# Products of the weights-stationary jobs sent in four runs of one width per block, and a lock for holders of several 512-column slots

## The chip, the cores and the metric

The kernel runs on one core of a Trainium2 chip. The metric is the time of one execution in device microseconds (us); less is better. The comparison is with the kernel before, whose median over three runs is 1254.39 us. Two engines matter most here: TensorE (PE in the profile), which multiplies, with its weight loads shown as PEld; and VectorE (DVE), which does the additions, differences and sums between the products. ScalarE (ACT) copies, rounds and applies functions; SyncE (SP) starts the transfers of the weights.

## The reference

Two layers of a decoder trunk over 256 positions and 1024 channels, in float32. Each layer is a mixer and a feed-forward part:

```python
u = rmsnorm(h) @ w_in                       # q, k, v, g, z, xbc, dt and two gates
yr = retention(rotary(q), rotary(k), v)      # 4 heads, chunks of 128
o_ret = (silu(g) * yr * rsqrt(mean(yr**2))) @ ret_out
xs, bm, cm = split(silu(causal_dwconv(xbc)))
ys = ssd_scan(xs * dt, dt * a, bm, cm)       # 4 groups of 8 heads, chunks of 128
o_ssd = (norm(ys + d_skip * xs, silu(z))) @ ssd_out
h = h + (sigmoid(gr) * o_ret + sigmoid(gs) * o_ssd) @ w_o
h = h + (silu(f @ w_gate) * (f @ w_up)) @ w_down     # f = rmsnorm(h)
```

and a last rmsnorm. Nearly all of the arithmetic is in the products with weights, some 260 MB of which are read once.

## The kernel before

**Products.** Every float32 operand of a large product is split into a high part (`wh` of a weight piece, `xh` of an activation) and the rest (`wl`, `xl`), and three products stand for one: high by high, high by low, low by high. In most jobs the activations are the stationary operand and TensorE streams 512 columns of weights three times (`mm3`, L541 to L543).

**The weights-stationary jobs** (`fm_job`, L971) turn this round. They make the projections that are needed with channels on the partitions: bc, q, k and xs in the mixer, and part of gate and up in the feed-forward. The stationary operand is 128x128 of weights, and what is streamed is the activation `xT`, whose tile keeps high and low halves side by side (256 + 256 columns). So one product of 512 columns with `wh` gives high by high and high by low at once (L989, or L992 for the last), and one of 256 columns with `wl` gives low by high (L990), added into the first 256 columns of the same PSUM bank. A job has two blocks (`b`) of 128 output channels; a block is eight k-steps, each a 512 and a 256, in turn. Its weights come in two pieces (k 0 to 3 and k 4 to 7), each of which must have been split by ScalarE (`wh`, L504) and VectorE (`wl`, L525). A layer has 30 such jobs (4 bc, 4 q, 4 k, 8 xs, 10 in the feed-forward), so the program has 60 jobs and 120 blocks.

**What sets the order.** While the program is built, a planner (`Flow`, L72) plays all engines on a clock of its own. Work is written as streams, which ask for operations with a cost and a priority, for events and for slots (`Sem`). Whenever an engine is free, its ready operation of lowest priority number is emitted (`run`, L157). Each engine's order is thereby fixed at build time; on the chip every engine runs its own list, and waits for the others by semaphores. A k-step of `fm_job` is one operation of the planner (L995), and transposes, scores or the products of another stream can be put between two of them.

**512-column slots.** `sxS` (L262) has four buffers of 128x512. Several kinds of work take more than one at a time. `seven_sums` (L673) makes the sums of operand quarters that a seven-product scheme needs; where it has no ready copies (its `plain` is None), it fills all four (`plain<-Y` in the profile) and makes from them four sums (`plain<-plain`), each split in two. `ssd_chunk` (L1683) of the state-space scan takes two, `xdt` and `tail`, for each of the two chunks of a group; the first chunk's `xdt` is kept until the second has used it. Single slots go to the convolution (L1614), the retention scores (L1460) and `copied` (L905).

Of the kernel before, what the change touches and what calls it, by code (L numbers as in the profile page):

```python
# [18 lines left out]
SEQ = 256  # L19
# [173 lines left out]
def trunk_kernel(  # L193
# [35 lines left out]
    def tt(n, pr, out, in0, in1, op):  # L229
        return dve(n, pr, lambda: nc.vector.tensor_tensor(out=out, in0=in0, in1=in1, op=op))  # L230
# [14 lines left out]
    def pe(cost, pr, fn):  # L245
        return Op("pe", cost, fn, pr)
# [5 lines left out]
    def pooled(pool_, shape, dt, tag, bufs):  # L252
        sem = Sem(bufs)
        return sem, lambda name=tag: pool_.tile(list(shape), dt, tag=tag, name=name, bufs=bufs)
# [5 lines left out]
    ccS, new_cc = pooled(tp, (P, D), F32, "cc", 2)  # L260
    silS, new_sil = pooled(tp, (P, 512), F32, "sil", 3)
    sxS, new_sx = pooled(tp, (P, 512), F32, "sx", 4)  # L262
    segS, new_seg = pooled(tp, (P, HPG, P), F32, "seg", 2)
    wbS, new_wb = pooled(tp, (P, D), F32, "wb", 1)
    decS, new_dec = pooled(tp, (P, D), F32, "dec", 2)
# [407 lines left out]
    def seven_sums(ops, op, parts, tag, pr, plain=None):  # L673

        p, r = parts
        for q, n, t in (("11", p, 0), ("21", r, 0), ("t4", r, 1)):
            yield op.ready[n][t]
            fl.set(ops[q], tuple(a[:, :, t * P : (t + 1) * P] for a in op.at(n)[:2]))
        x = {}
        for n in range(2):  # L680
            for t in range(NT):
                yield (plain[n][t] if plain else op.ready[parts[n]][t])
        for n in range(2):
            for t in range(NT):
                if plain:
                    x[n, t] = yield plain[n][t]
                else:
                    xh, xl = (a[:, :, t * P : (t + 1) * P] for a in op.at(parts[n])[:2])
                    yield sxS
                    x[n, t] = new_sx("plain")  # L690
                    v = x[n, t].rearrange("p (j t) -> p j t", j=4)
                    yield tt(512, pr, v, xh.bitcast(F32), xl.bitcast(F32), ALU.add)
        x11, x12, x21, x22 = x[0, 0], x[1, 0], x[0, 1], x[1, 1]
        pair = None
        for i, (q, out, a, b, op_) in enumerate((
                ("t1", x22, x21, x22, ALU.subtract), ("t2", x22, x22, x11, ALU.subtract),
                ("22", x12, x12, x22, ALU.add), ("t3", x21, x11, x21, ALU.subtract))):
            yield tt(512, pr, out, a, b, op_)
            if i % 2 == 0:
                yield bigS[tag]  # L700
                yield bigS[tag]
                pair = new_big(tag, F32R), new_big(tag, F32R)
            sh, sl = (p[:, :, (i % 2) * P : (i % 2 + 1) * P] for p in pair)
            v = out.rearrange("p (j t) -> p j t", j=4)
            yield act(512, pr, sh, v, AF.Copy)
            yield tt(512, pr, sl, v, sh.bitcast(F32), ALU.subtract)
            fl.set(ops[q], (sh, sl))
        for _ in range(4):
            fl.release(sxS)
# [261 lines left out]
    def fm_job(xT, post):  # L971

        j, pe_pr = take()
        evs = jobs[j]
        second = Event()
        for b in range(2):
            fsl = slice(b * P, (b + 1) * P)
            yield accS
            ps = None
            for k in range(8):  # L980
                for t in range(NT):
                    yield xT.ready[k // 4][t]
                wh, wl = yield evs[k // 4]

                def emit():
                    a = new_acc() if ps is None else ps
                    xh, _, x = xT.at(k // 4)
                    if k < 7:
                        nc.tensor.matmul(a, lhsT=wh[:, k % 4, fsl], rhs=x[:, k % 4, :, :], start=k == 0, stop=False)  # L989
                    nc.tensor.matmul(a[:, :SEQ], lhsT=wl[:, k % 4, fsl], rhs=xh[:, k % 4, :], start=False, stop=False)  # L990
                    if k == 7:
                        nc.tensor.matmul(a, lhsT=wh[:, k % 4, fsl], rhs=x[:, k % 4, :, :], start=False, stop=True)  # L992
                    return a

                ps = yield pe(mm_cost(512) + mm_cost(256) + 5, pe_pr + 0.5, emit)  # L995
                if b == 1 and k % 4 == 3:
                    fl.release(hlS)
            if b == 0:
                fl.spawn(post(ps, second, j))
            else:  # L1000
                fl.set(second, ps)
# [260 lines left out]
    def layer(l, mix, nxt, opening=None):  # L1262
# [420 lines left out]
        def ssd_chunk(g, t, lp, pr, dtt, acs, dec, dr, prm, cb, xs, x0_ev):  # L1683
# [18 lines left out]
            yield Op("act", HPG * (0.833 * P + 185), differences, lp)  # L1702
            yield act(1024, lp, sg, sg, AF.Exp, scale=-1.0)
            yield tt(1024, lp, sg, sg, cb[:, 2 * t, :].unsqueeze(1).broadcast_to([P, HPG, P]), ALU.mult)
            yield sxS
            xdt = new_sx("xdt")
            yield tt(512, lp, h3(xdt), h3(xs[:, t, :]), hb(dtt, t * NH, g), ALU.mult)
            yield sxS
            tail = new_sx("tail")
            dsb = prm[:, 2, g * HPG : (g + 1) * HPG].unsqueeze(2).broadcast_to([P, HPG, HD])  # L1710
            yield tt(512, lp, h3(tail), h3(xs[:, t, :]), dsb, ALU.mult)
# [562 lines left out]
```

## Time and profile before

| | us |
|---|---|
| median of three runs | 1254.39 (1253.65 to 1254.71) |
| the profiled execution | 1252.77 |
| its span, first to last instruction | 1251.0 |
| TensorE busy | 1241.2 (99%) |
| VectorE busy | 1109.2 (89%) |
| ScalarE busy | 883.5 (71%) |

The profile is of one execution. A matmul's record lasts from its start to its modelled end, and the next starts before that, so mean durations overlap; what a matmul costs in a stream is the distance from its start to the next start. In a timeline the columns are start, duration (both us), engine, line, operation and operands. In groups they are the count, the busy time in us, the mean duration in ns, and the idle time before with what ended it. Lines (L...) are those of the kernel before.

### The profile page before, as it was taken

The page shows a single profiled execution, that of the slowest core. Times are in us where ns is not written, and L with a number is a line of the kernel's source. Part 1 is how long each engine was busy: PE and PEld are TensorE (multiplying, and loading weights), DVE is VectorE, ACT ScalarE, POOL GpSimd, SP SyncE. Part 2 cuts the span into 40 slices and gives each one's busy share as a digit, 9 for nine tenths or more (in the row PEclk, how much of TensorE's full clock was granted, in tenths as well). Part 3 has the DMA queues.
Part 4 walks back from the last instruction along what each step waited for, and adds up shares of the span by engine and source line. Part 5 has one row for each costly group of instructions (what it writes and reads, how often), then busy time and mean ns, then how long its engine had stood idle before and what let it go on. Part 6 is the DMA issues. An engine that isn't in the chain of part 4 may idle for free.

```text
span 1251.0 us, 17642 instructions
## 1 busy us (share of the span) xinstructions
PE 1241.2 (99%) x6301; PEld 1052.5 (84%) x6301; DVE 1109.2 (89%) x1520; ACT 883.5 (71%) x1307; POOL 71.1 (6%) x92
## 2 busy tenths in 40 slices
PE   9999999999999999999999999999999999999997
PEld 8889888888888888888888898888888888888886
DVE  6998989789999979999788888888899998889996
ACT  6866876977776666776586676878877674776753
POOL 0000000001012001001000000000010110010000
PEclk9999999999999999999999999999999999999999
DMA  8758555466768658877776574555576786678872
GB/s 300 246 141 284 184 181 173 153 199 187 252 239 224 230 178 230 295 217 218 250 255 225 123 259 163 189 170 163 210 187 234 243 234 213 217 212 254 292 201 88
DMA packets 76343, 266.27 MB, mean 213 GB/s; under 512 B 8768, under 2 KB 9280, under 8 KB 76256
## 3 DMA queue, kind: packets, MB, share of 16 engines
q1 hardware_dynamic: 68416, 237.39, 55.1%
q0 software_dynamic: 7552, 27.38, 11.7%
q8 instruction: 49, 0.80, 0.3%
q10 hardware_dynamic: 288, 0.39, 0.1%
q14 instruction: 38, 0.31, 0.1%
HBM read 262.96 MB, written 2.16 MB: 212 GB/s over the span
## 4 chain that ended last, share of the span: by engine, by line
PE 88%; ACT 4%; issue 3%; DMA 3%; DVE 2%; POOL 0%; SPq 0%; POOLq 0%; ACTq 0%; DVEq 0%
PE acc L541 19%; PE acc L543 19%; PE acc L542 18%; PE acc L989 14%; PE acc L990 8%; PE tr L638 2%; PE yps L1731 2%; PE acc L992 2%; ACT wh L504 2%; DMA raw<-in_w_fm_dram 1%; DMA raw<-in_w_tm_dram 1%; DVE wl L525 1%; ACT seg L1699 1%; PE acc L1453 1%; PE tr L1624 1%
## 5 line engine op out<-in xcount | busy, mean ns | idle before, releaser
L504 ACT ACTIVATE wh<-raw 128x1024 fp32r<-128x1024 f32 (+2 forms) x388 | 397.0, 1035 | 148.6 <-PE acc L543 33.2
L525 DVE TENSOR_TENSOR wl<-raw,wh 128x1024 fp32r<-128x1024 f32 (+2 forms) x388 | 457.9, 1193 | 48.2 <-ACT wh L504 46.3
L989 PE MATMUL acc<-xT,wh 128*128 128x512 f32 x840 | 304.1, 400 | 0.0
L990 PE MATMUL acc<-xT,wl 128*128 128x256 f32 x960 | 251.6, 281 | 0.0
L541 PE MATMUL acc<-wh,xT 128*128 128x512 f32 (+1 forms) x568 | 220.5, 388 | 0.0
L543 PE MATMUL acc<-wh,xT 128*128 128x512 f32 (+1 forms) x568 | 216.1, 381 | 0.0
L542 PE MATMUL acc<-wl,xT 128*128 128x512 f32 (+1 forms) x568 | 216.1, 380 | 0.0
L990 PEld LDWEIGHTS acc<-xT,wl 128*128 128x128 f32 x960 | 181.2, 189 | 10.1
L989 PEld LDWEIGHTS acc<-xT,wh 128*128 128x128 f32 x840 | 158.0, 188 | 32.1
L542 PEld LDWEIGHTS acc<-wl,xT 128*128 128x128 f32 x568 | 106.8, 188 | 20.5 <-issue 1.2
L541 PEld LDWEIGHTS acc<-wh,xT 128*128 128x128 f32 x568 | 106.8, 188 | 19.8 <-issue 1.6
L543 PEld LDWEIGHTS acc<-wh,xT 128*128 128x128 f32 x568 | 106.6, 188 | 19.4
L504 ACT ACTIVATE wh<-raws 128x1024 fp32r<-128x1024 f32 x80 | 83.6, 1057 | 32.3 <-DVE raws L230 11.3
L525 DVE TENSOR_TENSOR wl<-raws,wh 128x1024 fp32r<-128x1024 f32 x80 | 96.2, 1219 | 8.6 <-ACT wh L504 8.4
L541 PE MATMUL acc<-wh,A 128*128 128x512 f32 x224 | 89.8, 401 | 0.3
L543 PE MATMUL acc<-wh,A 128*128 128x512 f32 x224 | 87.4, 390 | 0.0
L542 PE MATMUL acc<-wl,A 128*128 128x512 f32 x224 | 87.3, 390 | 0.0
L233 DVE SCALAR_TENSOR_TENSOR cc<-cc,cv 128x255 f32<-128x255 f32 (+1 forms) x144 | 67.0, 476 | 3.0 <-ACT cc L223 2.1
L541 PE MATMUL acc<-wh,C 128*128 128x512 f32 (+2 forms) x155 | 59.7, 385 | 0.0
L542 PE MATMUL acc<-wl,C 128*128 128x512 f32 (+2 forms) x155 | 58.9, 380 | 0.4 <-DVE wl L525 0.4
L543 PE MATMUL acc<-wh,C 128*128 128x512 f32 (+2 forms) x155 | 58.8, 379 | 0.0
L223 ACT ACT_TABLE_LOAD x41 | 52.6, 1283 | 6.0 <-DVE cc L233 5.3
(197 smaller groups left out, 2008.1 us busy)
## 6 DMA issues: line engine op xcount, KB each, us to landing
raw<-in_w_tm_dram SPq DMA_DIRECT2D x104, 512.0 KB, 4.2
raw<-in_w_fm_dram SPq DMA_DIRECT2D x80, 512.0 KB, 4.1
raw<-in_w_gf_dram SPq DMA_DIRECT2D x40, 512.0 KB, 4.6
raw<-in_w_gate_up_dram SPq DMA_DIRECT2D x32, 512.0 KB, 5.9
raw<-in_w_down_dram SPq DMA_DIRECT2D x28, 512.0 KB, 4.6
raw<-in_w_gr_dram SPq DMA_DIRECT2D x24, 352.0 KB, 3.4
seg<-acs SPq DMA_DIRECT2D x16, 512.0 KB, 4.8
raw<-in_ret_out_dram SPq DMA_DIRECT2D x16, 512.0 KB, 4.3
```

The costliest lines, as they stand in the source:

```text
L223: return Op("act", cost, lambda: nc.scalar.activation(out=out, in_=in_, func=func, **kw), pr, TABLES.get(func))
L233: return Op("dve", 1.04 * n + 130, lambda: nc.vector.scalar_tensor_tensor(out=out, in0=in0, scalar=scalar, in1=in1, op0=op0, op1=op1), pr)
L504: nc.scalar.activation(out=wh[:, :m], in_=raw[:, :m], func=AF.Copy)
L525: nc.vector.tensor_tensor(out=wl[:, :m], in0=raw[:, :m], in1=wh[:, :m].bitcast(F32), op=ALU.subtract)
L541: nc.tensor.matmul(ps, lhsT=lh, rhs=rh, start=first, stop=False, **kw)
L542: nc.tensor.matmul(ps, lhsT=lh, rhs=rl, start=False, stop=False, **kw)
L543: nc.tensor.matmul(ps, lhsT=ll, rhs=rh, start=False, stop=last, **kw)
L638: nc.tensor.transpose(out=ps[:, j * P : (j + 1) * P], in_=src[:, j * P : (j + 1) * P], identity=ident)
L989: nc.tensor.matmul(a, lhsT=wh[:, k % 4, fsl], rhs=x[:, k % 4, :, :], start=k == 0, stop=False)
L990: nc.tensor.matmul(a[:, :SEQ], lhsT=wl[:, k % 4, fsl], rhs=xh[:, k % 4, :], start=False, stop=False)
L992: nc.tensor.matmul(a, lhsT=wh[:, k % 4, fsl], rhs=x[:, k % 4, :, :], start=False, stop=True)
L1731: nc.tensor.matmul(ps[:, i * HD : (i + 1) * HD], lhsT=sg[:, i, :], rhs=xdt[:, i * HD : (i + 1) * HD], start=True, stop=True)
```

## The change

Three things change in the code.

- In `fm_job` a block's products are sent in four runs: the four 512s of the first piece, its four 256s, the four 256s of the second piece, and its four 512s. Each run is given to the planner as two operations of two products each, and the planner's cost for them has 5 ns added for a pair of 512s and none for a pair of 256s (it was 5 ns for each 512 with its 256). A weight piece is given back at the same place as before, after its eighth product in the second block.
- A lock `sxG` with one holder. `seven_sums` takes it, where it has no ready copies, before its four slots, and gives it back when it has filled all four.
- `ssd_chunk` takes the same lock in a group's first chunk ahead of `xdt`, and it is given back in the second chunk when that has its second slot.

Nothing is added to or taken from the arithmetic: the numbers of products, additions and transfers are the same.

```diff
     sxS, new_sx = pooled(tp, (P, 512), F32, "sx", 4)
+    sxG = Sem(1)
...
             for t in range(NT):
                 yield (plain[n][t] if plain else op.ready[parts[n]][t])
+        if not plain:
+            yield sxG
...
                     yield tt(512, pr, v, xh.bitcast(F32), xl.bitcast(F32), ALU.add)
+        if not plain:
+            fl.release(sxG)
...
             yield accS
-            ps = None
-            for k in range(8):
+            box = []
+            for half, wide in ((0, True), (0, False), (1, False), (1, True)):
                 for t in range(NT):
-                    yield xT.ready[k // 4][t]
-                wh, wl = yield evs[k // 4]
-
-                def emit():
-                    a = new_acc() if ps is None else ps
-                    xh, _, x = xT.at(k // 4)
-                    if k < 7:
-                        nc.tensor.matmul(a, lhsT=wh[:, k % 4, fsl], rhs=x[:, k % 4, :, :], start=k == 0, stop=False)
-                    nc.tensor.matmul(a[:, :SEQ], lhsT=wl[:, k % 4, fsl], rhs=xh[:, k % 4, :], start=False, stop=False)
-                    if k == 7:
-                        nc.tensor.matmul(a, lhsT=wh[:, k % 4, fsl], rhs=x[:, k % 4, :, :], start=False, stop=True)
-                    return a
-
-                ps = yield pe(mm_cost(512) + mm_cost(256) + 5, pe_pr + 0.5, emit)
-                if b == 1 and k % 4 == 3:
+                    yield xT.ready[half][t]
+                wh, wl = yield evs[half]
+
+                def emit(k0):
+                    if not box:
+                        box.append(new_acc())
+                    xh, _, x = xT.at(half)
+                    for k in (k0, k0 + 1):
+                        if wide:
+                            nc.tensor.matmul(box[0], lhsT=wh[:, k, fsl], rhs=x[:, k, :, :],
+                                             start=(half, k) == (0, 0), stop=(half, k) == (1, 3))
+                        else:
+                            nc.tensor.matmul(box[0][:, :SEQ], lhsT=wl[:, k, fsl], rhs=xh[:, k, :], start=False, stop=False)
+
+                for k0 in (0, 2):
+                    yield pe(2 * mm_cost(512 if wide else SEQ) + (5 if wide else 0), pe_pr + 0.5, lambda: emit(k0))
+                if b == 1 and (half, wide) in ((0, False), (1, True)):
                     fl.release(hlS)
...
             yield act(1024, lp, sg, sg, AF.Exp, scale=-1.0)
+            if t == 0:
+                yield sxG
             yield sxS
             xdt = new_sx("xdt")
...
             yield sxS
+            if t == 1:
+                fl.release(sxG)
             tail = new_sx("tail")
```

How the change moves instructions is seen in the order in which each engine's list is emitted. Operands in it are named as in the profile, and a number after a name tells buffers apart. In the changed kernel's list L996 and L999 are the 512s and the 256s of `fm_job`, and L526 is the split that was L525.

TensorE, the first block of the first bc job, before: `wh_418` and `wl_459` are the first piece's high and low part, `wh_446` and `wl_470` the second's.

```order
L989 MATMUL acc_502<-xT_317,wh_418 128x512
L990 MATMUL acc_502<-xT_317,wl_459 128x256
L989 MATMUL acc_502<-xT_342,wh_446 128x512
L990 MATMUL acc_502<-xT_342,wl_470 128x256
L990 MATMUL acc_502<-xT_342,wl_470 128x256 x2
L992 MATMUL acc_502<-xT_342,wh_446 128x512
```

Of the rows that repeat one stands here; in the list the first two come four times and the next two three times. The same block and the next one in the changed kernel:

```order
L996 MATMUL acc_502<-xT_317,wh_418 128x512 x4
L999 MATMUL acc_502<-xT_317,wl_459 128x256 x4
L999 MATMUL acc_502<-xT_342,wl_470 128x256 x4
L996 MATMUL acc_502<-xT_342,wh_446 128x512 x4
L996 MATMUL acc_537<-xT_317,wh_418 128x512 x4
L999 MATMUL acc_537<-xT_317,wl_459 128x256 x4
L999 MATMUL acc_537<-xT_342,wl_470 128x256 x4
L996 MATMUL acc_537<-xT_342,wh_446 128x512 x4
```

The width changes fourteen times inside a block before, and twice in the changed kernel; from one block to the next 512 follows 512 in both.

VectorE in layer 0, where the retention's sums begin and the second chunk of a state-space group ends, before: `plain<-Y` fills a slot for `seven_sums`, `xdt<-ips`, `tail<-tail` and `C<-yps` belong to the chunk, `wl<-raw` splits a weight piece, `sil<-A` and `A<-tr` make the retention's output.

```order
L230 TENSOR_TENSOR xdt<-ips,sr 128x512
L230 TENSOR_TENSOR tail<-tail,xdt 128x512
L233 SCALAR_TENSOR_TENSOR sil<-A,rr_2068,sil 128x512
L230 TENSOR_TENSOR plain<-Y 128x512
L233 SCALAR_TENSOR_TENSOR sil<-A,rr_2068,sil 128x512
L525 TENSOR_TENSOR wl<-raw,wh 128x1024
L230 TENSOR_TENSOR C<-yps,tail 128x512
L230 TENSOR_TENSOR plain<-Y 128x512
L230 TENSOR_TENSOR A<-tr,A 128x4x128
L230 TENSOR_TENSOR plain<-Y 128x512 x2
```

The same place in the changed kernel, from the same first row on:

```order
L230 TENSOR_TENSOR xdt<-ips,sr 128x512
L230 TENSOR_TENSOR tail<-tail,xdt 128x512
L230 TENSOR_TENSOR Y<-tr,Y 128x4x128
L233 SCALAR_TENSOR_TENSOR cc<-cc,cv 128x255
L230 TENSOR_TENSOR plain<-Y 128x512
L233 SCALAR_TENSOR_TENSOR cc<-cc,cv 128x254
L526 TENSOR_TENSOR wl<-raw,wh 128x1024
L233 SCALAR_TENSOR_TENSOR cc<-cc,cv 128x253
L526 TENSOR_TENSOR wl<-raw,wh 128x1024
L230 TENSOR_TENSOR cc<-acc,cc 128x256
L230 TENSOR_TENSOR C<-yps,tail 128x512
L230 TENSOR_TENSOR plain<-Y 128x512
```

The chunk's product sum `C<-yps` is still behind the first slot that `seven_sums` fills, with more convolution rows and one more weight split between; the four fills are drawn out over more of VectorE's list.

More of the change, by code (lines that the diff above doesn't have):

```diff
@@ L978, in fm_job @@
             yield accS
-            ps = None
-            for k in range(8):
+            box = []
+            for half, wide in ((0, True), (0, False), (1, False), (1, True)):
                 for t in range(NT):
-                    yield xT.ready[k // 4][t]
-                wh, wl = yield evs[k // 4]
-                def emit():
-                    a = new_acc() if ps is None else ps
-                    xh, _, x = xT.at(k // 4)
-                    if k < 7:
-                        nc.tensor.matmul(a, lhsT=wh[:, k % 4, fsl], rhs=x[:, k % 4, :, :], start=k == 0, stop=False)
-                    nc.tensor.matmul(a[:, :SEQ], lhsT=wl[:, k % 4, fsl], rhs=xh[:, k % 4, :], start=False, stop=False)
-                    if k == 7:
-                        nc.tensor.matmul(a, lhsT=wh[:, k % 4, fsl], rhs=x[:, k % 4, :, :], start=False, stop=True)
-                    return a
-                ps = yield pe(mm_cost(512) + mm_cost(256) + 5, pe_pr + 0.5, emit)
-                if b == 1 and k % 4 == 3:
+                    yield xT.ready[half][t]
[13 more added lines that the diff above has]
+                if b == 1 and (half, wide) in ((0, False), (1, True)):
                     fl.release(hlS)
+            ps = box[0]
             if b == 0:
```

## The prediction

> **What bounds the kernel now.** I read the page first: which engine is full, and whether its clock is held back.
>
> ```profile
> PE 1241.2 (99%) x6301; PEld 1052.5 (84%) x6301; DVE 1109.2 (89%) x1520; ACT 883.5 (71%) x1307; POOL 71.1 (6%) x92
> PEclk9999999999999999999999999999999999999999
> ```
>
> TensorE is busy 99% of the span at full granted clock. Then the waits, of TensorE and of its weight loads, since a busy share can hide short stops:
>
> ```profile
> PE idle L2147 <- DVE mhalf L2124: 1.3, 1, 1.3
> PE tr L638 <- DVE sil L233: 0.9, 3, 0.3
> PE acc L542 <- DVE wl L525: 0.4, 2, 0.2
> PE acc L1453 <- DVE C L230: 0.3, 1, 0.3
> PEld acc L541 <- ACT sil L223: 2.0, 4, 0.5
> PEld acc L542 <- DVE wl L525: 1.2, 3, 0.5
> ```
>
> The first four are all the waits listed for TensorE: 2.9 us, of which 1.3 is the start. So the time is the sum of what the products cost in the stream, and little can be won but by making that cost less. The groups say how much of the stream the change touches:
>
> ```profile
> L989 PE MATMUL acc<-xT,wh 128*128 128x512 f32 x840 | 304.1, 400 | 0.0
> L990 PE MATMUL acc<-xT,wl 128*128 128x256 f32 x960 | 251.6, 281 | 0.0
> L992 PE MATMUL acc<-xT,wh 128*128 128x512 f32 x120 | 47.6, 397 | 0.0
> ```
>
> 960 products of 512 and 960 of 256 columns, eight of each in every one of 120 blocks. The means here (400 and 281 ns) hold the tail of one product that the next overlaps; the cost in the stream is read from starts in the timeline.
>
> **The runs of one width.** First what a block costs now. These are the first products of four blocks that follow each other in the feed-forward with nothing between:
>
> ```profile
> 484.39 0.40 PE L989 MATMUL acc<-xT,wh 128*128 128x512 f32 x1
> ...
> 487.21 0.40 PE L989 MATMUL acc<-xT,wh 128*128 128x512 f32 x1
> ...
> 490.03 0.40 PE L989 MATMUL acc<-xT,wh 128*128 128x512 f32 x1
> ...
> 492.85 0.40 PE L989 MATMUL acc<-xT,wh 128*128 128x512 f32 x1
> ```
>
> (492.85 - 484.39) / 3 = 2.82 us for a block. Next what the same products cost where widths do not mix. A stretch of 512s of the seven-product scheme, its first and last row, 62 products apart:
>
> ```profile
> 499.76 0.39 PE L541 MATMUL acc<-wh,D 128*128 128x512 f32 x1
> ...
> 513.81 0.39 PE L543 MATMUL acc<-wh,xT 128*128 128x512 f32 x1
> ```
>
> (513.81 - 499.76) / 62 = 0.2266 us each. And the one stretch of 256s that this kernel has, in its last job, with the 512 ahead of it:
>
> ```profile
> 1240.49 0.39 PE L543 MATMUL acc<-wh,Y 128*128 128x512 f32 x1
> 1240.71 0.28 PE L541 MATMUL acc<-wh,C 128*128 128x256 f32 x1
> 1240.83 0.28 PE L542 MATMUL acc<-wl,C 128*128 128x256 f32 x1
> ...
> 1241.07 0.28 PE L541 MATMUL acc<-wh,C 128*128 128x256 f32 x1
> ...
> 1244.07 0.28 PE L542 MATMUL acc<-wl,Y 128*128 128x256 f32 x1
> ```
>
> 25 products from 1241.07 to 1244.07: 0.1200 us each. Unmixed, a block would be 8 x 226.6 + 8 x 120.0 = 2773 ns; mixed it is 2820. The difference, 47 ns, comes with fourteen changes of width, so 3.4 ns a change. Two changes are left, so 12/14 of 47 = 40 ns go if each change costs the same; up to 47 go if the two at the ends of a run cost nothing, for which the rows above speak: 512 to 256 took 0.22 us there, and the first 256 was no slower than those after it.
>
> Not every block pays the 47 ns. After a transpose or scores the alternation can settle on a shorter beat; this block, from its first product to the next block's first, took 2.78 us:
>
> ```profile
> 815.64 0.39 PE L989 MATMUL acc<-xT,wh 128*128 128x512 f32 x1
> ...
> 818.42 0.39 PE L989 MATMUL acc<-xT,wh 128*128 128x512 f32 x1
> ```
>
> Going through the timeline I estimate that a sixth of the 120 blocks run like this. There 7 ns or so are to be had, not 40 to 47. So 100 blocks x 40 to 47 ns + 20 x 0 to 7 ns = 4.0 to 4.8 us; I take 4.4, in the middle. The bounds of the unknown: at the least nothing, if the 47 ns have another cause; at the most 120 x 47 = 5.6 us.
>
> The Trainium skill, page "TensorE: Matmul & The Clock Gate", section "Back-to-back issue gap", gives a gap that depends on a product's own width alone, N / 2.4 + 2.5 ns at full clock. By it, as an estimate, the eight pairs cost 2.60 us in either order and the change is worth nothing; the trace has more than that formula for both widths, and a mixed block that costs more than its parts.
>
> **When the weights are wanted.** The first piece's `wl` is now wanted after four 512s, 0.9 us into a block (before: after one, 0.23 us), and the second piece's `wl` ahead of its `wh`, so 0.23 us earlier than before. What hides that is the lead of the splits. TensorE's waits above name `wl` twice, for 0.4 us in all, and at L542, a line of `mm3`; L990 is not among them, nor among those of the weight loads. Price: 0. If that lead were gone, it would be up to 60 x 0.23 = 14 us. The changed order also lets other streams in only between pairs of one width; a transpose in the middle of a run costs two more changes of width at most where it falls inside alternation before anyway. Price: 0, by 7 ns a time either way.
>
> **The lock.** It adds no instruction. `plain is None` holds for three kinds of sums in a layer: the retention's, the state-space's and the down projection's. What waits at the lock in the planner is a stream, not an engine, so nothing stands queued behind it on VectorE; but its rows are emitted later or drawn out. These are the rows that it governs:
>
> ```profile
> L230 DVE TENSOR_TENSOR plain<-Y x20: 681/683/686, 259.7 to 1191.8; 128x512 f32<-128x512 f32 x20
> L230 DVE TENSOR_TENSOR xdt<-C,dtt 128x512 f32<-128x512 f32 x16 | 10.9, 682 | 0.0
> L230 DVE TENSOR_TENSOR tail<-C,prm 128x512 f32<-128x512 f32 x16 | 10.9, 681 | 0.0
> ```
>
> At the place shown from the order, the first `plain<-Y` stands behind the same chunk's `tail<-tail` in both kernels, and the chunk's last sum behind it in both; between, the changed list has a weight split and convolution rows more. That is about 2 us later for the group's result, which is read only by the z jobs, long after the q, k and xs jobs that are running there. Price: 0, from below -0.5 (a shorter wait somewhere) to +1 us. On ScalarE the changed order has six fewer table loads, 36 instead of 42 in the lists; each is this row's 1283 ns:
>
> ```profile
> L223 ACT ACT_TABLE_LOAD x41 | 52.6, 1283 | 6.0 <-DVE cc L233 5.3
> ```
>
> ScalarE is 71% busy, so those 7.7 us are off the path; they can at best remove part of the 2.0 us that weight loads waited for `sil`. SP's transfers of weights keep their order among themselves; `seg` loads trade places with a few of them, with nothing waiting on those in the lists above.
>
> **The sum.** The profiled execution took 1252.77 us: the span of 1251.0 and 1.77 around it, which does not change. 1252.77 - 4.4 = 1248.4. The median of the runs, 1254.39, lies 1.62 above that profile, and the same step from it gives 1250.0.
>
> **The rivals.** *VectorE takes the gain back.* The stages behind the projections are nearly full on VectorE:
>
> ```profile
> 300.00:350.00 50.00, 50.00 (x244) 41.85 (x243) 48.91 (x61) 35.59 (x53) 3.39 (x5) 1.00 0.77 236
> 350.00:400.00 50.00, 50.00 (x244) 41.49 (x243) 49.05 (x66) 33.23 (x50) 9.03 (x12) 1.00 0.72 231
> 950.00:1000.00 50.00, 50.00 (x248) 41.74 (x247) 49.01 (x68) 31.17 (x46) 4.81 (x8) 1.00 0.66 227
> ```
>
> (the columns after the length are busy us of PE, PEld, DVE, ACT and POOL.) VectorE works 49 of 50 us there while TensorE still never stops. If TensorE arrives earlier by what the 40 mixer blocks of a layer save and then waits for splits, 80 x 37 ns = 3.0 us are given back and 1.4 remain: 1253.0. For it: the 98%. Against: TensorE is at 50.00 in the same rows, and the work VectorE has there was partly laid down earlier and moves with it.
>
> *The 47 ns are not from the change of width.* Then the streams differ by operand or bank, nothing is won, and it stays at 1254.4. For it: the sixth of the blocks that alternate and yet take 2.78 us. Against: their products are the same, of the same operands, so operands do not explain the difference. This is also what the skill page's gap rule, named above, would give.
>
> *Slower: the drawn-out sums hold the slots.* `seven_sums` now fills its four slots over some eighteen rows of VectorE's list, where it took seven, and meanwhile the retention's scores and the convolutions lack a slot. If the first sums' products were late by the whole of the four fills, the four sums and the four rests, 12 x 0.683 = 8.2 us a layer, the program would be 16.4 - 4.4 = 12 us slower: 1266. It turns the sign when TensorE waits over 2.2 us a layer. Against: `A<-tr`, on which the last quarter of the same job depends, keeps its place among these rows in both lists.
>
> **How the numbers follow.** My forecast has 0.70, VectorE taking it back 0.12, no effect of width 0.10, the slots 0.05, and 0.03 is left for waits of another kind. About 0.2% (2.5 us) is what a measurement of this kernel can tell from no change: faster means below 1251.9, slower above 1256.9. The forecast's own bounds, 4.0 to 5.6 saved with waits of -0.5 to +1, are 1248.3 to 1251.4, nearly all of it faster; the first two rivals fall within 0.2%. With some of the forecast's weight moved over for waits that I can't see: faster 0.74, same 0.20, slower 0.06. The range runs from 1247.6, where small waits go too, to 1253.4, which takes in the first rival and leaves out the others.
>
> **What would show it.** Right: blocks that follow each other start 2.77 to 2.78 us apart; in a run the 256s start 0.120 and the 512s 0.227 us apart; TensorE's waits stay near 3 us; TensorE's busy time falls by 4 to 5 us with the span. Wrong: 256s in a run that start further apart than 0.120, for which the weight load would be the first suspect; waits of L541 or L542 for `wl` in the stages from 300 and 950 us on; waits for `O` or `A` ahead of the retention's output products.

## The result, and the profile after

The changed kernel takes 1256.95 us (median; 1255.18 to 1258.63), the kernel before beside it 1253.61 (1252.84 to 1254.72). The ratio is 1.0025, with a 95% interval of 1.0016 to 1.0034: slower, by some 3.3 us, where 4.4 us faster was forecast. The profiled execution took 1256.67 us, its span 1254.4.

The first part of the page after, and its row of the granted clock:

```profile
PE 1241.8 (99%) x6301; PEld 1052.7 (84%) x6301; DVE 1108.5 (88%) x1520; ACT 874.9 (70%) x1301; POOL 77.2 (6%) x92
PEclk9999999999999999999999999999999999999999
```

TensorE is as busy as before and at full clock, so the loss is not there to be seen. What TensorE waits for shows it (line, what ended the wait and on which engine; then us in all, times, the longest):

```profile
PE idle L2159 <- DVE mhalf L2136: 1.3, 1, 1.3
PE acc L542 <- ACT sx L223: 1.2, 2, 1.0
PE tr L639 <- DVE D L230: 1.1, 2, 0.6
PE ips L1730 <- DVE xdt L230: 1.1, 2, 0.6
PE tr L639 <- DVE sil L233: 0.8, 2, 0.5
PE acc L542 <- DVE cc L230: 0.3, 1, 0.3
PE acc L1461 <- DVE C L230: 0.2, 1, 0.2
```

6.0 us are listed where 2.9 were. New are `sx`, `D` and `xdt`, each once in either layer, and once `cc`. The first three lie behind the mixers' projections. To see what that stage costs I take its first product after the last block of `fm_job` and the first product of the feed-forward's first block. In layer 1 they stand in the timeline of before so:

```profile
890.85 0.40 PE L541 MATMUL acc<-wh,xT 128*128 128x512 f32 x1
...
1089.99 0.39 PE L989 MATMUL acc<-xT,wh 128*128 128x512 f32 x1
```

and in that of the changed kernel so:

```profile
891.62 0.39 PE L542 MATMUL acc<-wh,xT 128*128 128x512 f32 x1
...
1094.13 0.39 PE L996 MATMUL acc<-xT,wh 128*128 128x512 f32 x1
```

199.14 us became 202.51. In layer 0 the same stage went from 199.14 (273.15 to 472.29) to 201.63 (272.37 to 474.00). The two stages, which hold none of the products that the change rearranges, lost 2.5 + 3.4 = 5.9 us.

The runs of one width did gain. Three rows of the changed kernel's timeline, over one whole block from the second half of one to the second half of the next (a row stands for as many products as its last column says, and begins with the first):

```profile
1108.05 2.00 PE L996 MATMUL acc<-xT,wh 128*128 128x512 f32 x8
1109.89 1.12 PE L999 MATMUL acc<-xT,wl 128*128 128x256 f32 x8
1110.84 2.00 PE L996 MATMUL acc<-xT,wh 128*128 128x512 f32 x8
```

Eight 512s take 1.84 us, eight 256s 0.95, a block 2.79 us. The median over blocks that follow each other without anything between is 2793 ns after and 2819 before: 26 ns a block, 3.1 us over 120 blocks, not 40 to 47 ns a block. So the balance of these two is 5.9 - 3.1 = 2.8 us lost. Two smaller terms stand at the end of the program. Behind the last block of `fm_job` the span is 0.3 us shorter (63.7 us, 64.0 before). But an execution of the changed kernel takes 2.2 us more than its span (the profiled one 1256.67 - 1254.4 = 2.27), one of the kernel before 1.8 (1252.77 - 1251.0 = 1.77): 0.4 us that no trace shows and whose cause was not followed. With both, 2.9 us are lost; the 0.4 us left to the measured 3.3 lie within what the start of the program varies by (see the end).

### The profile page after: what moved, and what is told of

It is laid out like the page before. It is cut to its first block, busy times and chain, and to the rows that moved or that the text cites. A ratio compares the mean times of both kernels' runs of the same rounds, so it can differ in the third digit from the quotient of the medians.

```text
span 1254.4 us, 17632 instructions
## 1 busy us (share of the span) xinstructions
PE 1241.8 (99%) x6301; PEld 1052.7 (84%) x6301; DVE 1108.5 (88%) x1520; ACT 874.9 (70%) x1301; POOL 77.2 (6%) x92
## 4 chain that ended last, share of the span: by engine, by line
PE 82%; DVE 6%; DMA 5%; issue 3%; ACT 3%; POOL 0%; SPq 0%; POOLq 0%; DVEq 0%; ACTq 0%
PE acc L542 17%; PE acc L544 17%; PE acc L543 17%; PE acc L996 16%; PE acc L999 8%; DVE wl L526 3%; PE tr L639 2%; PE yps L1743 2%; DMA raw<-in_w_rw_dram 2%; ACT wh L505 1%; DMA raws<-in_w_sw_dram 1%; DMA raw<-in_w_gr_dram 1%; DMA raw<-in_w_fm_dram 1%; PE acc L1461 1%; PE tr L1632 1%
## 5 line engine op out<-in xcount | busy, mean ns | idle before, releaser
L526 DVE TENSOR_TENSOR wl<-raw,wh 128x1024 fp32r<-128x1024 f32 (+2 forms) x388 | 459.4, 1197 | 52.1 <-ACT wh L505 49.9
L996 PE MATMUL acc<-xT,wh 128*128 128x512 f32 x960 | 249.5, 395 | 0.0
L542 PE MATMUL acc<-wh,xT 128*128 128x512 f32 (+1 forms) x568 | 221.1, 389 | 0.0
L543 PE MATMUL acc<-wl,xT 128*128 128x512 f32 (+1 forms) x568 | 216.3, 381 | 0.0
L996 PEld LDWEIGHTS acc<-xT,wh 128*128 128x128 f32 x960 | 171.2, 189 | 29.0
L999 PEld LDWEIGHTS acc<-xT,wl 128*128 128x128 f32 x960 | 131.3, 190 | 9.8 <-issue 0.5
L999 PE MATMUL acc<-xT,wl 128*128 128x256 f32 x960 | 136.7, 283 | 0.0
L543 PEld LDWEIGHTS acc<-wl,xT 128*128 128x128 f32 x568 | 106.8, 188 | 20.9 <-issue 1.2
L542 PEld LDWEIGHTS acc<-wh,xT 128*128 128x128 f32 x568 | 106.7, 188 | 20.4 <-issue 1.6
L526 DVE TENSOR_TENSOR wl<-raws,wh 128x1024 fp32r<-128x1024 f32 x80 | 96.8, 1222 | 8.7 <-ACT wh L505 8.3
L542 PE MATMUL acc<-wh,A 128*128 128x512 f32 x224 | 88.9, 397 | 0.4 <-DVE cc L230 0.3
L543 PE MATMUL acc<-wl,A 128*128 128x512 f32 x224 | 87.2, 389 | 0.0
L542 PE MATMUL acc<-wh,C 128*128 128x512 f32 (+2 forms) x155 | 59.4, 383 | 0.0
L543 PE MATMUL acc<-wl,C 128*128 128x512 f32 (+2 forms) x155 | 58.8, 380 | 0.1
```

Source lines behind the costliest of these rows:

```text
L526: nc.vector.tensor_tensor(out=wl[:, :m], in0=raw[:, :m], in1=wh[:, :m].bitcast(F32), op=ALU.subtract)
L542: nc.tensor.matmul(ps, lhsT=lh, rhs=rh, start=first, stop=False, **kw)
L543: nc.tensor.matmul(ps, lhsT=lh, rhs=rl, start=False, stop=False, **kw)
L996: nc.tensor.matmul(box[0], lhsT=wh[:, k, fsl], rhs=x[:, k, :, :], start=(half, k) == (0, 0), stop=(half, k) == (1, 3))
L999: nc.tensor.matmul(box[0][:, :SEQ], lhsT=wl[:, k, fsl], rhs=xh[:, k, :], start=False, stop=False)
```

## The experiments

The changed kernel mixes two things: products in runs, and the order that the planner makes of everything under the new costs. They can be had apart. Theory A: the order costs the time. Rival B: VectorE, which is nearly full in the stage, takes the gain back whenever TensorE comes early. A table of all runs stands at the end of this part.

**Runs in the old order.** The products of the changed kernel, each of the eight operations of a block with the cost of the old pair, no lock. Every other instruction stands in its list as before.

```diff
-    sxG = Sem(1)
...
-                    yield pe(2 * mm_cost(512 if wide else SEQ) + (5 if wide else 0), pe_pr + 0.5, lambda: emit(k0))
+                    yield pe(mm_cost(512) + mm_cost(256) + 5, pe_pr + 0.5, lambda: emit(k0))
```

> The products of a block in four runs of one width, but each of the eight operations at the planner's old cost, and no lock. All other engines' lists, and TensorE's outside these jobs, are then row for row those of before. Theory A (the changed kernel lost its gain to a new order of all engines' work, which its new planner costs brought about): the waits of the changed kernel at the state-space product near 357 and 976 us, at the retention's products near 326 and 946 us and at the transposes near 423 and 1043 us are gone, blocks start 2.79 us apart, 120 x 27 ns = 3.2 us are saved: 1250.4 us, ratio 0.9974 (0.9968 to 0.9982). Rival B (TensorE only reaches the stages in which VectorE is full earlier, and waits there in any order): the same waits are there, ratio 0.999 to 1.003.

1250.65 us, ratio 0.998 [0.9971, 0.9989]. All that TensorE waits for in this kernel:

```profile
PE idle L2150 <- DVE mhalf L2127: 1.3, 1, 1.3
PE tr L638 <- DVE sil L233: 0.6, 2, 0.3
PE acc L542 <- DVE wl L525: 0.5, 1, 0.5
PE acc L541 <- ACT wh L504: 0.2, 1, 0.2
```

The stage takes 199.17 us in both layers (271.66 to 470.83, 888.22 to 1087.39), as before, though TensorE arrives 1.5 and 2.6 us earlier. The ratio is in A's range (0.9968 to 0.9982). B falls, and what the blocks save is kept to the end: 2.7 of the 3.1 us by the medians.

**The new order without runs.** The changed kernel's costs, lock and lists, with 512 and 256 in turn inside a block again.

```diff
-                    for k in (k0, k0 + 1):
-                        if wide:
+                    k = k0 // 2 + (0 if wide == (half == 0) else 2)
+                    last = (half, k) == (1, 3)
+                    if not last:
...
```

> The changed kernel with its planner costs, its lock and so its order of all engines' work, but a 512 and a 256 in turn inside each block as before. A: the waits stay and the 3.2 us of the runs are lost as well: 1259 to 1260.5 us, ratio 1.0045 to 1.0055. B: TensorE arrives as late as before, the waits go: ratio 0.999 to 1.001.

1258.32 us, ratio 1.0042 [1.003, 1.0055], a block 2819.5 ns, and the stage takes 201.50 and 202.43 us. The ratio is just under A's 1.0045 to 1.0055 and far from B's 0.999 to 1.001. So the order without the runs costs 5.3 us by the ratio, and the runs give their part back in either order.

**A third order.** All eight operations of a block at one cost, the mean of the new ones.

```diff
+                    yield pe(349.2, pe_pr + 0.5, lambda: emit(k0))
```

> The changed kernel with all eight operations of a block at the same planner cost of 349.2 (a block's measured 2.79 us shared out evenly): a third order, unlike both others in all engines' lists. A: 3.2 us of the runs are saved, and what waits this order brings is its own matter; by the two orders known, between 0 and 6 us of them: 1250 to 1256 us, and whichever it is the blocks are 2.79 us apart. B: like the changed kernel, 1256 to 1258 us, with waits at the same places.

1256.83 us, ratio 1.0025 [1.0015, 1.0036]. It loses as much, but elsewhere: 3.3 us in five waits for `wl` at L543, 201.90 and 202.52 us in the stage. A had 1250 to 1256 us, B 1256 to 1258 us with the waits at the same places: the time is out of A's range, and the places are not B's. This order is no better than the changed kernel's.

**Runs of two in the old order.** Two 512s, two 256s and so on, to see what a change of width costs.

```diff
+                    at = k0 // 2 + (0 if wide == (half == 0) else 2)
+                    for k in (at // 2 * 2, at // 2 * 2 + 1):
+                        if at % 2 == half:
```

> The order of before, with the products in twos of one width inside a block: 512 512 256 256 512 512 256 256, then 256 256 512 512 256 256 512 512. Six changes of width in a block, three of them back to 512. If each change costs the same 3.4 ns: a block takes 2773 + 6 x 3.4 = 2.793 us, and about 1250.5 us in all. If it is the return to 512 that costs, 6 to 10 ns on each of the first products after it, with 7 ns given back at the first 256: 2.80 to 2.81 us a block, 1251.5 to 1252.5 us in all.

1251.31 us, ratio 0.9983 [0.9974, 0.9993]; a block takes 2800 ns. Six changes at 3.4 ns each on 2773 would be 2793. Start to start, a block in the changed kernel without interruption runs 231, 227, 226, 227 | 113, then seven of 120 | 233, 236, 228, 233 ns. A change from 512 to 256 costs nothing (the first 256 is even 7 ns short), but a return to 512 makes the next five products slow: 233 + 236 + 228 + 233 + 231 is 28 ns over five of 226.6. It is the return that has a price, and it takes five products to be paid in full, which a run of two cuts short. The price is not always asked: in the kernel before, 90 blocks have nothing between their sixteen products, and six of them took 2777 to 2788 ns with seven returns each (the prediction shows one, at 815.64 us), at most some 2 ns a return. What decides this was not found.

**The new costs in the feed-forward only.**

```diff
+    def fm_job(xT, post, ffn=False):
...
+                    yield pe((2 * mm_cost(512 if wide else SEQ) + (5 if wide else 0)) if ffn else (mm_cost(512) + mm_cost(256) + 5), pe_pr + 0.5, lambda: emit(k0))
```

> The changed kernel, but with the new planner costs for the feed-forward's jobs alone; the mixers' jobs have the old cost (the products of all jobs go in runs). TensorE's list outside these jobs is that of before, VectorE's differs in a few rows. Theory A (the order that the mixers' new costs brought is what costs): the waits near 326, 357, 423 us and near 946, 976, 1043 us are gone, the runs save what they save in the old order: 1250 to 1251.5 us, ratio 0.9975 to 0.9985. Rival C (the new costs are bad wherever they stand, since 458 and 240 in place of 352 make the planner put other work at worse points): half of the loss or so stays, 1252.5 to 1254.5 us.

1251.29 us, ratio 0.998 [0.997, 0.9989]; the stage takes 199.20 and 199.34 us. It is the costs in the mixers that bring the loss.

**A little more or less on the cost.** The cost of each operation is the old one plus 0.5, minus 0.5, or plus 2 ns, with the lock. It changes nothing in the program but the order.

```diff
+                    yield pe(mm_cost(512) + mm_cost(256) + 5 + 0.5, pe_pr + 0.5, lambda: emit(k0))
```

> Runs of one width, the lock, and the old cost plus 0.5 ns for each of a block's eight operations. Such a difference says nothing of the work, but it gives another order from the middle of the program on. A': any other order than that of before draws its own lot of waits, between none and some 6 us: 1250.5 to 1257 us, and waits of TensorE stand in the profile for whatever is above 1250.6. C: the costs are nearly the old ones, so the order is as good: 1250 to 1251.5 us.

1260.52 us, ratio 1.0045 [1.0032, 1.0058].

> The same with the old cost less 0.5 ns, again another order. A': between 1250.5 and 1257 us, with waits for whatever is above 1250.6, and not the time of the order that plus 0.5 ns gives but by chance. C: 1250 to 1251.5 us.

1266.59 us, ratio 1.0094 [1.0081, 1.0106].

> The same with the old cost plus 2 ns, which gives an order that differs in nearly as many rows as the changed kernel's. A': between 1250.5 and 1257 us, with waits for whatever is above 1250.6. C: 1250 to 1251.5 us.

1254.75 us, ratio 1.0008 [0.9999, 1.0017]. Half a nanosecond in an operation of a third of a microsecond costs 8 or 14 us by the ratios, against the same products in the old order. C, by which the order stays as good (1250 to 1251.5 us), falls three times. A' holds for the last kernel alone: the first two lie above its 1257 us. Each order has stops of its own. The worst of them, in the timeline of the kernel with half a nanosecond less:

```profile
323.15 0.39 PE L544 MATMUL acc<-wh,Y 128*128 128x512 f32 x1
326.31 2.04 PE L1730 MATMUL ips<-xdt,cbm 128*128 128x512 f32 x2 [2.78 <-DVE xdt L230]
328.91 0.79 PE L542 MATMUL acc<-wh,Y 128*128 128x512 f32 x1 [0.56 <-ACT sx L223]
```

and windows around it (length, TensorE busy us and products, granted clock, DMA share, GB/s):

```profile
316.00:326.00 10.00, 7.53 (x42) 0.99 0.91 330
326.00:330.00 4.00, 3.13 (x5) 0.50 0.88 329
330.00:334.00 4.00, 4.00 (x19) 0.50 0.28 87
334.00:338.00 4.00, 4.00 (x14) 0.75 0.84 280
338.00:342.00 4.00, 4.00 (x19) 1.00 0.10 40
```

The two stops are listed with 2.78 + 0.56 = 3.3 us, and the clock is at half from 326 to 336 us (the 0.75 is the mean over a window in whose middle it comes back): 10 x 0.5 = 5 us more. Together that is about the 8.2 us by which this layer's stage is longer (207.31 us). The Trainium skill, page "TensorE: Matmul & The Clock Gate", section "Part 1: The HAM clock gate", has TensorE fall to half clock after an idle window of about 3.4 us; here a stop listed with 2.78 us was enough. The stops of 1.0 us in the changed kernel left the clock at 1.00.

**More lead.** Theory D: the planner lets TensorE's operations follow too closely on what VectorE and ScalarE make, so that small errors of its clock become stops; 500 or 1000 ns more in its table would take the stops away. Rival E: it is a draw, and more lead is only another order.

```diff
-        "act": {"pe": 271.0, "act": 153.0, "dve": 142.0, "pool": 170.0, "sp": 100.0},
-        "dve": {"pe": 256.0, "act": 128.0, "dve": 127.0, "pool": 155.0, "sp": 100.0},
+        "act": {"pe": 771.0, "act": 153.0, "dve": 142.0, "pool": 170.0, "sp": 100.0},
+        "dve": {"pe": 756.0, "act": 128.0, "dve": 127.0, "pool": 155.0, "sp": 100.0},
```

> The changed kernel, with the planner's time from an end on VectorE or ScalarE to a start on TensorE raised by 500 ns (from 256 and 271), so that it puts products that wait for those engines later in TensorE's list. Theory D (an order loses time where it leaves TensorE's product too little behind the VectorE or ScalarE row that it needs; the waits of the changed kernel are 0.3 to 1.0 us long): most of those waits go, 1250.5 to 1253.5 us. Rival E (the order is a matter of chance, and a lead gives one more draw): anywhere from 1250.5 to 1266 us, with waits as long as before at other places.

1257.35 us, ratio 1.0036 [1.0024, 1.0047].

> The same with 1000 ns. D: all those waits go, 1250.5 to 1252 us, unless buffers that are held longer stop something else. E: anywhere from 1250.5 to 1266 us.

1279.18 us, ratio 1.0202 [1.0189, 1.0216]; `sx` alone is waited for 12.3 us.

> The kernel with the old cost less 0.5 ns, the slowest order found (1266.6 us, with two waits of 2.8 us for the state-space rows), with a lead of 500 ns. D: the two long waits are shortened by about 0.5 us each or go: under 1262 us. E: anywhere from 1250.5 to 1266 us.

1254.23 us, ratio 0.9999 [0.9991, 1.0008].

> The same with 1000 ns. D: lower than with 500 ns, under 1258 us, and no wait over 1.8 us. E: anywhere from 1250.5 to 1266 us, not in the order of the leads.

1276.19 us, ratio 1.0181 [1.0168, 1.0194]. D falls: 500 ns took nothing off the one order and 12 us off the other, and 1000 ns made both far worse. E fits the two kernels with 500 ns; those with 1000 ns lie beyond its 1266 us too. That buffers held longer stop something else, as the second expectation allowed, would fit the waits for `sx`, 12.3 us here and 9.7 us in the last kernel; it was not tested.

**Single rows.** What makes a stop? Around 945 us the changed kernel's ScalarE and TensorE run so, each in its timeline:

```profile
941.86 1.05 ACT L505 ACTIVATE wh<-raw 128x1024 fp32r<-128x1024 f32 x1
942.92 1.28 ACT L223 ACT_TABLE_LOAD   x1
944.22 1.06 ACT L223 ACTIVATE seg<-seg 128x1024 f32<-128x1024 f32 x1
945.18 0.58 ACT L223 ACTIVATE sx<-acc 128x512 f32<-128x512 f32 x1
```

```profile
944.41 0.39 PE L544 MATMUL acc<-wh,Y 128*128 128x512 f32 x1
945.81 0.50 PE L542 MATMUL acc<-wh,Y 128*128 128x512 f32 x1 [1.01 <-ACT sx L223]
```

The next job's first product needs the bank that the copy `sx<-acc` empties, and ahead of the copy stand an exp and the table load that it needs, 2.3 us. In before, the table load (935.26) and the exp (936.55) begin 7.4 us ahead of the copy (942.70) instead of 2.3, with five splits between. So theory G: the loss is single rows that stand just wrong. Rival H: VectorE and ScalarE are late as a whole, and a stop that is taken away comes back further on. These kernels hold a row back until the next instruction of its engine is sent, while the planner's clock goes on as if it had been sent; every list but for the traded rows stays as it was.

```diff
+    def send(self, kind, eng, which, fn):
+        n = self.nth[kind] = self.nth.get(kind, -1) + 1
+        if n in which:
+            self.held[eng] = [2, fn]
+        else:
+            fn()
...
+            ex = act(1024, lp, sg, sg, AF.Exp, scale=-1.0)
+            fn = ex.fn
+            ex.fn = lambda: fl.send("exp", "act", (6, 14), fn)
```

> The changed kernel with two ScalarE rows traded in each layer and every other list row for row as it was: the copy sx<-acc goes ahead of the exp seg<-seg and its table load, behind which it stands just before the stops at 326.01 and 945.81 us of the changed kernel's trace (table load 1.28 us and exp 1.06 us ahead of a copy of 0.57 us). Theory G, the loss is made of single rows that stand too early or too late: both stops go and nothing takes their place. Worked out from starts in the changed kernel's trace, the stop at 326.01 costs 0.55 + 0.34 - 2 x 0.227 = 0.44 us and that at 945.81 costs 1.40 + 0.34 - 2 x 0.227 = 1.29 us, so 1.7 us: the difference to the kernel before falls from 3.3 to 1.6 us, ratio 1.0013. Rival H, VectorE and ScalarE are late as a whole in these stages and the stop only shows where: the wait turns up some products later, listed waits stay near 6 us, ratio stays at 1.0025.

1255.76 us, ratio 1.0017 [1.0008, 1.0026]. ScalarE at the same place:

```profile
942.77 1.04 ACT L519 ACTIVATE wh<-raw 128x1024 fp32r<-128x1024 f32 x1
943.72 0.58 ACT L237 ACTIVATE sx<-acc 128x512 f32<-128x512 f32 x1
944.32 1.28 ACT L237 ACT_TABLE_LOAD   x1
945.61 1.06 ACT L237 ACTIVATE seg<-seg 128x1024 f32<-128x1024 f32 x1
```

No wait for `sx` is left, and the two stages take 0.83 + 0.85 = 1.7 us less, as G has it in sum (by the ratios 1.0 us). In layer 0 it is more than G's 0.44, since the transposes of `D` stop for 0.24 instead of 0.63 us; in layer 1 less than 1.29, since a wait of 0.63 us for `wl` appeared at 957.43. The listed waits stay at 6.2 us, as H has it, but by two more waits for `wl` (0.9 us), at 20.59 and 93.28 us, that lie far ahead of the stages.

The second kernel of this kind moves four places of TensorE's list behind the three products that follow: `ips` and the first transposes of `D`, in each layer.

```diff
+                    fl.send("ips", "pe", (3, 7), lambda: nc.tensor.matmul(ps, lhsT=cb[:, 1, :], rhs=x0, start=True, stop=True))
...
+            fl.send("tr", "pe", (20, 54), turn)
```

> The changed kernel with four places of TensorE's list changed and every other list row for row as it was: the product ips<-xdt,cbm at 356.30 and 976.17 us of the changed kernel's trace, and the transposes tr<-cst,D at 423.27 and 1042.99 us, go behind the three products that follow them (0.68 us). Theory G: each finds its operand then, the stops go but for about 0.1 us, 4 x 0.68 less 0.05 = 2.7 us; the difference to the kernel before falls from 3.3 to 0.6 us, ratio 1.0005. Rival H: VectorE is the bound there, its next row is then waited for instead, and the ratio stays at 1.0025.

1255.42 us, ratio 1.0017 [1.0008, 1.0026]. The two stages take 1.7 us less, not 2.7. The stops at `ips` went; those at the transposes moved on by one group and grew (0.77 and 0.65 us). For `ips`, the changed kernel's TensorE and VectorE had shown why:

```profile
355.40 0.39 PE L544 MATMUL acc<-wh,xT 128*128 128x512 f32 x1
356.30 1.10 PE L1730 MATMUL ips<-xdt,cbm 128*128 128x512 f32 x2 [0.52 <-DVE xdt L230]
```

```profile
355.47 0.69 DVE L230 TENSOR_TENSOR xdt<-xdt,sr 128x512 f32<-128x512 f32 x1
```

and the same two instructions in before:

```profile
357.19 1.02 PE L1718 MATMUL ips<-xdt,cbm 128*128 128x512 f32 x2
```

```profile
355.64 0.69 DVE L230 TENSOR_TENSOR xdt<-xdt,sr 128x512 f32<-128x512 f32 x1
```

VectorE reaches `xdt` at nearly the same time in both, but TensorE, with its last product begun at 355.40, would have come to `ips` at 355.63, 1.6 us earlier than in before. Of that it had 0.8 us at the beginning of the stage (272.37 against 273.15); the rest is the order.

> The changed kernel with all six places of the two kernels beside it. Theory G: the gains add up, 1.7 + 2.7 = 4.4 us, listed waits of TensorE fall from 6.0 to near 2.9 us or under, and the kernel is 1.0 us faster than the kernel before, ratio 0.9992 (0.998 to 1.0005). Rival H: ratio 1.0020 to 1.0030, and the listed waits stay near 6 us at other places of the same stages.

1254.85 us, ratio 1.0009 [1.0, 1.0018], between the ranges of G and H: the stages take 3.0 us less than in the changed kernel, where 4.4 were expected, and 5.2 us of waits are listed. At the transposes VectorE shows a split ahead of the difference `D<-D` that they wait for:

```profile
422.11 0.69 DVE L244 TENSOR_TENSOR D<-D 128x512 f32<-128x512 f32 x1
422.71 1.22 DVE L540 TENSOR_TENSOR wl<-raw,wh 128x1024 fp32r<-128x1024 f32 x1
423.85 0.69 DVE L244 TENSOR_TENSOR D<-acc,D 128x512 f32<-128x512 f32 x1
424.45 1.22 DVE L540 TENSOR_TENSOR wl<-raw,wh 128x1024 fp32r<-128x1024 f32 x1
425.58 0.69 DVE L244 TENSOR_TENSOR D<-D 128x512 f32<-128x512 f32 x1
```

The last of these kernels trades the last two rows, in both layers, besides.

```diff
+            fl.send("wl", "dve", (164, 414), lambda: nc.vector.tensor_tensor(
+                out=wl[:, :m], in0=raw[:, :m], in1=wh[:, :m].bitcast(F32), op=ALU.subtract))
```

> The kernel with six rows moved, and on VectorE one weight split wl<-raw traded in each layer with the difference D<-D behind it (in six_rows_moved the split stands at 424.45 us and takes 1.13 us to the next start, D<-D follows at 425.58, and the transposes that need it stop for 0.77 us at 426.41 in the trace's count of TensorE and for 0.59 us at 1044.77). Every other list stays row for row. Theory G: D<-D comes 1.13 us earlier, both stops go, worth 0.77 + 0.59 + 2 x 0.27 = 1.9 us with what a stop costs beside its listed time, and the ratio falls from 1.0009 to 0.9994 (0.9985 to 1.0003). Rival H, VectorE is late as a whole there: the transposes behind them or the split's own products stop instead, and the ratio stays at 1.0005 to 1.0015.

1254.31 us, ratio 1.0008 [0.9999, 1.0017]: no more than the six won, where G had 0.9994; it lies in H's range. The transposes no longer stop; 1.6 us later the next products do:

```profile
426.25 0.60 PE L656 MATMUL tr<-cst,D 128*128 128x128 f32 x4
...
427.81 0.50 PE L559 MATMUL acc<-wh,A 128*128 128x512 f32 x1 [0.49 <-DVE A L244]
```

Here H holds: VectorE shows no idle time between 418 and 430 us, and TensorE runs into whatever it makes next. At the copies and at `ips` G holds in the main. In all four kernels with moved rows the ratio falls by 0.7 to 1.0 us less than the stages, which are read from one execution each; why was not followed.

All runs, with the stage between the projections and the feed-forward from the traces, as above:

| kernel | layer 0, us | layer 1, us | ratio [95%] |
|---|---|---|---|
| before | 199.1 | 199.1 | |
| runs_old_order | 199.2 | 199.2 | 0.998 [0.9971, 0.9989] |
| pairs_old_order | 199.1 | 199.3 | 0.9983 [0.9974, 0.9993] |
| new_costs_feedforward_only | 199.2 | 199.3 | 0.998 [0.997, 0.9989] |
| the changed kernel | 201.6 | 202.5 | 1.0025 [1.0016, 1.0034] |
| alternate_new_order | 201.5 | 202.4 | 1.0042 [1.003, 1.0055] |
| runs_third_order | 201.9 | 202.5 | 1.0025 [1.0015, 1.0036] |
| runs_cost_plus_half | 199.2 | 207.8 | 1.0045 [1.0032, 1.0058] |
| runs_cost_minus_half | 207.3 | 207.1 | 1.0094 [1.0081, 1.0106] |
| runs_cost_plus_two | 201.4 | 199.6 | 1.0008 [0.9999, 1.0017] |
| new_costs_lead_500 | 202.9 | 201.0 | 1.0036 [1.0024, 1.0047] |
| new_costs_lead_1000 | 216.7 | 210.7 | 1.0202 [1.0189, 1.0216] |
| minus_half_lead_500 | 200.7 | 199.6 | 0.9999 [0.9991, 1.0008] |
| minus_half_lead_1000 | 211.7 | 210.1 | 1.0181 [1.0168, 1.0194] |
| copy_ahead_of_exp | 200.8 | 201.7 | 1.0017 [1.0008, 1.0026] |
| ips_and_transposes_later | 200.8 | 201.6 | 1.0017 [1.0008, 1.0026] |
| six_rows_moved | 200.4 | 200.7 | 1.0009 [1.0, 1.0018] |
| eight_rows_moved | 200.3 | 201.0 | 1.0008 [0.9999, 1.0017] |

The best kernel is the first, the change's products in the order of before. **The lock** alone is not in the table. Added to the kernel before, to the runs in the old order, or to those with half a nanosecond or two on the cost, it changes no row of any engine's list, so there it costs nothing. Under the changed costs it can't be left out: without it the planner ends with streams that wait for each other's slots. What it adds to the loss in that order was not tried and stays open.

## Why the prediction was wrong

**The step that failed** is the price of the order. The prediction gave "The lock" a price of 0, -0.5 to +1 us, from one place of VectorE's list; it gave the moved transfers "nothing waiting"; it put other streams that come in between the new pairs at 0, "by 7 ns a time either way"; and the changed costs of the operations, which bring the new order on all engines, it did not price at all. The order of the mixers is another one under the new costs, and that costs 5.9 us in two stages. About half of it, 3.0 us, is six rows of ScalarE and TensorE that stand a microsecond early or late. Of the 2.8 us that are left, VectorE's lateness at the `D` differences makes some 1.9 by the sum in the last expectation, and it did not go away by moving a row; waits of 0.3 to 0.6 us that are left were not followed. Slower had 0.06, and a mechanism of slots; it came through the order.

**The term that was mis-sized** is the 4.4 us of the runs. Its direction, the 256s at 0.120 us, the free step from 512 to 256 and the sum of 2773 ns for an unmixed block agree with the rows of the changed kernel. Wrong was that the 47 ns come in equal parts with fourteen changes, of which the last two might be free: a return to 512 costs some 28 ns over five products, of which the first 256 of a run gives 7 or 8 back. One return is left, so 20 ns stay and 26 are saved, in 120 blocks 3.1 us. Why the return has a price stays open, and not every block pays it. The row of the last job on which the step rested shows only 512 to 256, not the way back. A sixth of the blocks on the shorter beat was too many: it was six of 90. And the 1.77 us around the span, "which does not change", became 2.27. The gap rule of the Trainium skill (page "TensorE: Matmul & The Clock Gate", section "Back-to-back issue gap"), which that section gives for an isolated product and by which there was nothing to gain, differs from the trace: 2819 ns against 2793 for the same sixteen products.

**The rivals.** That VectorE takes the gain back, as it was put (TensorE comes early and waits for splits), falls with runs_old_order: 1.5 and 2.6 us earlier, and no wait more. The 98% of VectorE may have been a sign, though, that there was little room for another order; that is an argument and was not tested. That the width has no effect falls too. The lead of the splits was priced rightly: no wait of TensorE in the changed kernel is at `fm_job`'s own lines. So were the six table loads fewer, whose number meant nothing; but one of those that are left stands with its exp ahead of a copy, and the stop there costs 1.3 us.

**What the signs showed.** Of the signs named for right, the 256s came as said and the 512s did not, blocks came at 2.79 instead of 2.77 to 2.78, TensorE's busy time rose by 0.6 us instead of falling by 4 to 5, and the waits, 6.0 instead of near 3 us, named the failure. Those named for wrong, at L541 or L542 for `wl` and ahead of the retention's products for `O` or `A`, did not come.

## What to carry to other kernels

Where a planner sets the order, a change of a cost by half a nanosecond can change every engine's list: change the products and the costs apart, and time the products in the old order first. When the bound engine is 99% busy and its neighbour 98%, price a new order by measuring some, not from the one place that was looked at; here nine other orders of the mixers cost 2 to 29 us more in the two stages than the one of before. And compare lengths of stages between two products that both kernels have, since the waits that are listed are shorter than what they cost.

## What the runs showed of the hardware

- A return from a run of 256s to products of 512 columns costs about 28 ns, spread over five products (233, 236, 228, 233 and 231 ns against 226.6); the way to 256 costs nothing (113 ns, then 120). In six blocks of 90 before, returns cost almost nothing.
- A stop listed with 2.78 us cost 5 us more by 10 us at half the clock. In these traces eight stops were of 2.7 us or more (up to 6.45 us), and 0.4 us after each at the latest the granted clock was at half. Of three stops of 2.29 us one was followed by half clock, of those of 1.8 us and less none. A stretch at half lasted 3.4, 6.8 or 10.2 us.
- A listed wait is less than its price. The one at 945.81 is listed with 1.01 us; from start to start it cost 1.40 - 0.23 us, and the product behind it 0.11 more, in all 1.29.
- The first 272 us are not the same length in two executions of one list: kernels whose lists are the same up to there reached the stage of layer 0 at 272.37, 273.27, 273.69, 273.80 and 274.11 us, with waits for `wl` that come and go. A single trace tells nothing about a microsecond there; the stage behind it took 199.1 to 199.3 us in every kernel with the old order.
